# Sample value gathers behind the delta rule, norm weights spread by TensorE, later residual steps, and a pinned order of the last transposes

## The chip, the core and the metric

The kernel runs on one core of one Trainium2 chip. A core has TensorE (PE; its weight loads are shown apart as PEld), VectorE (DVE), ScalarE (ACT), GpSimd (POOL) and SyncE (SP), which work in parallel, each through its own instructions in order, and meet through semaphores. SP, ACT and POOL also issue DMA transfers. The metric is the device time of one execution in microseconds; the median of several executions is compared.

## What is computed

The reference is one step of a hybrid decoder layer for 1024 prompt tokens and for 8 sampled sequences of 4 tokens each, in float32, with a model width of 1024. Cut to what matters here:

```python
h = rmsnorm(x, norm_mix_w)
p = h @ w_in                      # q,k,v | conv input u | z | a, b | gate_A, gate_B
o_a = stick_breaking(q, k, v)     # 8 heads of 64; samples also over 256 cached positions
o_b = gated_delta(silu(conv(u)))  # 4 heads of 128, state 128x128, chunks of 64
m = sigmoid(g_a) * (o_a @ w_pa) + sigmoid(g_b) * (o_b @ w_pb)
x = x + m @ w_o
x = x + square(relu(rmsnorm(x, norm_mlp_w) @ w_up)) @ w_down
y = rmsnorm(x, norm_final_w)
```

The sampled sequences read cached keys and values through a page table (`cache_k[page_table]`, `cache_v[page_table]`): 16 pages of 128 rows, each row 512 numbers.

## The kernel before

All large products are made from three matmuls each (`dense`, L134 to L139: high part by high part, high by low, low by high), with 256 to 288 columns of tokens at a time. A planner orders the instructions: it simulates the engines, and places an instruction by its place in the program among those that it thinks ready; `tc.high_priority()` lifts a block, and `tc.issue_after(x)` puts instructions behind `x`. The order that it writes is then fixed for each engine.

The stages, in order of the program:

- **Start** (L76 to L220). Nine tiles `xn` of tokens are loaded on SP's queue, with three weight tiles `ws_u` between them and, behind the second tile, `nmb`, the mixing norm's weights broadcast to 128 partitions (L95). Five small loads go on ACT's queue, four of them into `vrow`, which TensorE transposes into `vec` (L156 to L159), from where all small weights are read. For each tile ACT squares it (L197), POOL takes the power (L199), DVE multiplies by the scale and `nmb` (L200), TensorE transposes (`xtp`, L208), and ACT and DVE split the result into `xh` and `xl`.
- **Prompt delta rule**, four heads (`gdn_head`, L386 to L571).
- **Sample delta rule** (L578 to L772). Cached keys and values are fetched by indirect gathers that POOL issues: `keys(s)` (L591) into `kg`, of which two buffers exist, followed by TensorE's transposes `dkt`; `values(s)` (L604) into `vg`, of which four exist. For sequences 0 to 3 both are called ahead of the delta rule. This stage's products of states with keys and queries, `dks` (L716 to L724), are 2 x 64 short matmuls; `dM`, `dMT` (L708 to L715) stand ahead of them. The gathered values are first read at L891.
- **Attention projections and attention** (L774 to L1144). `gate_steps` (L1032) compute the gates; the first 11 of 16 gate jobs precede the attention blocks, and the other five are cut into 20 steps and handed out as fills between attention blocks (`pipeline`, L1023). Nine residual steps (L1041) stand among the fills: each loads one tile of `x` again (`xr`), transposes it (`xrp`), and stores it transposed (`xs` to `xT_d`). The fills are listed at L1068 to L1074; a residual step follows gate steps 0, 2, 4, ..., 16.
- **Output projection, channel mixer** (L1153 to L1570).
- **Last products and final norm** (L1573 to L1636). Feature tiles of `w_down` products are added into eight tiles `ys`, in four stages of columns. For each stage the squares are summed (`sa`, and `sl` for the last feature tile), TensorE sums them over partitions (`pf`, L1618 and L1619), POOL takes the power (`fr`), and the tiles are transposed (`fin`, L1630), scaled, and stored.

Of the kernel before, what the change touches and what calls it, by code (L numbers as in the profile page):

```python
# [8 lines left out]
F32 = mybir.dt.float32  # L9
F32R = mybir.dt.float32r  # L10
I32 = mybir.dt.int32
I64 = mybir.dt.int64
AF = mybir.ActivationFunctionType
ALU = mybir.AluOpType
# [24 lines left out]
def hybrid_step(ctx, tc, x_prompt, x_sample, cache_k, cache_v, page_table, state_conv, state_ssm,  # L39
# [29 lines left out]
    def gtile(name):  # L69
        return psg.tile([P, 512], F32, tag="g", name=name)  # L70
# [7 lines left out]
    sctx = ExitStack()  # L78
    sp = pool("sp", 2, stack=sctx, side="right")
    nmb = sp.tile([P, D], F32, name="nmb", bufs=1)  # L80
    vrow = sp.tile([P, P], F32, name="vrow", bufs=1)
    nc.vector.memset(vrow, 0.0)
    nc.scalar.dma_start(vrow[8:16, :], norm_mlp_w.rearrange("o (k p) -> (o k) p", p=P))
    nc.scalar.dma_start(vrow[16:64, :], conv_w.rearrange("o j (i p) -> (o j i) p", p=P))
    nc.scalar.dma_start(vrow[64:65, :], gdn_norm_w)
    nc.scalar.dma_start(vrow[65:73, :], norm_final_w.rearrange("(k p) -> k p", p=P))
    winv = w_in[0].rearrange("(k p) n -> p k n", p=P)
    xns, w0s = [], []
    for t in range(9):
        xn = sp.tile([P, D], F32, tag="xn", name=f"xn{t}", bufs=7)  # L90
        n = P if t < 8 else NS
        SY.dma_start(xn[:n], x_prompt[0, t * P:(t + 1) * P, :] if t < 8 else x_sample.rearrange("s t d -> (s t) d"))
        xns.append(xn)
        if t == 1:
            SY.dma_start(nmb, norm_mix_w.to_broadcast([P, D]))  # L95
        if t in (1, 3, 5):
            wp = wpool if t == 1 else gw if t == 5 else sp
            st = wp.tile([P, 8, P], F32, tag="wst", name=f"ws_u0{t}", bufs=1)
            col = {1: 2048, 3: 1536, 5: 2560}[t]
            SY.dma_start(st, winv[:, :, col:col + P])  # L100
            w0s.append(st)
    ident = cst.tile([P, P], F32, name="ident")
    make_identity(nc, ident)
    ones = cst.tile([P, P], F32, name="ones")
    V.memset(ones, 1.0)
    powc = cst.tile([P, 2], F32, name="powc")
    V.memset(powc[:, 0:1], -0.5)
    V.memset(powc[:, 1:2], 0.5)

    def tr(out, in_, k=P):  # L110
        PE.transpose(out, in_, ident[:k, :k])
# [41 lines left out]
    ms_d = dr.tile([GH, 4, NC, 32, 32], F32, name="ms_d")  # L153
    tv_d = dr.tile([GH, 4, NC, 32, 32], F32, name="tv_d")

    vps = gtile("vps")  # L156
    tr(vps[:, :P], vrow)
    vec = cst.tile([P, P], F32, name="vec")
    V.tensor_copy(vec, vps[:, :P])  # L159
    mlw = vec[:, 8:16]  # L160

    def cwv(j, i):
# [29 lines left out]
    for t in range(9):  # L192
        n = P if t < 8 else NS
        c0 = t * P
        xn = xns[t]
        junk = sp.tile([P, D], F32, tag="junk", name=f"junk{t}", bufs=1)
        S_.activation(junk[:n], xn[:n], AF.Square, accum_out=sst_[:n, t:t + 1])  # L197
        V.tensor_scalar(sst_[:n, t:t + 1], sst_[:n, t:t + 1], 1.0 / D, EPS, op0=ALU.mult, op1=ALU.add)
        rpow(rstd[:n, t:t + 1], sst_[:n, t:t + 1], 0, 1)  # L199
        V.scalar_tensor_tensor(xn[:n], xn[:n], rstd[:n, t:t + 1], nmb[:n], op0=ALU.mult, op1=ALU.mult)  # L200
        cc = min(t // 2, 3)
        co = c0 - CX[cc][0]
        for hf in range(2):
            pt = (ttile, gtile)[hf](f"xtp{t}_{hf}")
            pv = pt.rearrange("p (k c) -> p k c", k=4)
            for k in range(4):
                kk = hf * 4 + k
                tr(pv[:, k, :n], xn[:n, kk * P:(kk + 1) * P], n)  # L208
            xh_ = xhc[cc][:, hf * 4:hf * 4 + 4, co:co + n]
            S_.activation(xh_, pv[:, :, :n], AF.Copy)  # L210
            V.tensor_tensor(xlc[cc][:, hf * 4:hf * 4 + 4, co:co + n], pv[:, :, :n], xh_.bitcast(F32), op=ALU.subtract)
        if t in (1, 3, 5):
            w0.append(load_w(None, f"u0{t}", gw if t == 5 else wpool, w0s[t // 2]))
    scp = sp.tile([24, 1536], F32, name="scp", bufs=1)
    nc.scalar.dma_start(scp, state_conv[0].rearrange("s j c -> (s j) c"))
    pcv = gtile("pcv")
# [387 lines left out]
    def values(s):  # L604
        vgs[s] = bk.tile([P, 2, 512], F32, tag="vg", name=f"vg{s}", bufs=4)
        for pg in range(2):
            G.indirect_dma_start(vgs[s][:, pg, :], None, cvf, bass.IndirectOffsetOnAxis(ap=idx[:, 2 * s + pg:2 * s + pg + 1], axis=0))

    for s in range(4):
        keys(s)  # L610
        values(s)
    dctx = ExitStack()
    dk = pool("dk", stack=dctx, side="right")
    blkf = blk.rearrange("p b t -> p (b t)")
# [97 lines left out]
    pmt = gtile("dmt")  # L712
    tr(pmt[:, 0:P], dM)
    dMT = dk.tile([P, P], F32, name="dMT")
    V.tensor_copy(dMT, pmt[:, 0:P])  # L715
    pks = gtile("dks")  # L716
    for i, i0 in enumerate((4, 0)):
        kz = dk.tile([P, GH, NSEQ, NS], F32, tag="big", name=f"kz{i}")
# [322 lines left out]
    def residual_step(t):  # L1041
        n = P if t < 8 else NS
        xn = ak.tile([P, D], F32, tag="xr", name=f"xr{t}", bufs=1)
        SY.dma_start(xn[:n], x_prompt[0, t * P:(t + 1) * P, :] if t < 8 else x_sample.rearrange("s t d -> (s t) d"))
        for hf in range(2):
            pv = dtile(f"xrp{t}_{hf}", True).rearrange("p (k c) -> p k c", k=4)
            xs = ak.tile([P, 4, P], F32, tag="xs", name=f"xs{t}{hf}", bufs=1)
            for k in range(4):
                kk = hf * 4 + k
                tr(pv[:, k, :n], xn[:n, kk * P:(kk + 1) * P], n)  # L1050
            S_.activation(xs[:, :, :n], pv[:, :, :n], AF.Copy)
            SY.dma_start(xT_d[hf * 4:hf * 4 + 4, :, t * P:t * P + n].rearrange("k p c -> p k c"), xs[:, :, :n])
# [16 lines left out]
    for x, (j, b) in enumerate(gjobs[11:]):  # L1069
        for c in range(len(CX)):  # L1070
            fills.append(lambda j=j, b=b, c=c: gate_step(j, b, c))
            t = 4 * x + c
            if t % 2 == 0 and t // 2 < 9:
                fills.append(lambda t=t // 2: residual_step(t))  # L1074
    pipeline(0, SPLIT, fills)
    ofb0 = zp.tile([P, 4, 256], F32, tag="zz", name="ofb0")
    SY.dma_start(ofb0, o_d[4:8, :, 0:256].rearrange("k p c -> p k c"))
# [514 lines left out]
    for c, tiles in enumerate(stages):  # L1592
        o, o2 = c * QN, c % 2 * QN
        for j in range(KT):
            cs_ = slice(j * P, (j + 1) * P)
            pt = bk2[j % 2](f"pv{c}_{j}")
            hs = hid[c // 2]
            dense(pt, [w[:, 0, cs_] for w in wd], [w[:, 1, cs_] for w in wd], [h[:, 0, o2:o2 + QN] for h in hs],
                  [h[:, 1, o2:o2 + QN] for h in hs], QN)
            yv_ = ys[j][:, o:o + QN]  # L1600
            with tc.high_priority():
                V.tensor_tensor(yv_, pt[:, :QN], yv_, op=ALU.add)
            if j == 0:
                S_.activation(sa[:, o:o + QN], yv_, AF.Square)
            else:
                sb_ = lp.tile([P, QN], F32, tag="sb", name=f"sb{c}_{j}") if j < KT - 1 else sl[:, o:o + QN]
                S_.activation(sb_, yv_, AF.Square)
                if j < KT - 1:
                    V.tensor_tensor(sa[:, o:o + QN], sa[:, o:o + QN], sb_, op=ALU.add)
            S_.activation(yv_, yv_, AF.Copy, scale=vec[:, 65 + j:66 + j])  # L1610
        with tc.high_priority():
            pf = bk2[0](f"pf{c}")
            fr = lp.tile([P, 3], F32, tag="fr", name=f"fr{c}", bufs=2)
            V.memset(fr, 1.0)
            m = len(tiles)
            for i, t in enumerate(tiles):
                n = P if t < 8 else NS
                PE.matmul(pf[:n, i:i + 1], lhsT=sa[:, t * P:t * P + n], rhs=ones[:, 0:1], start=True, stop=False)  # L1618
                PE.matmul(pf[:n, i:i + 1], lhsT=sl[:, t * P:t * P + n], rhs=ones[:, 0:1], start=False, stop=True)  # L1619
            V.tensor_scalar(fr[:, 0:2], pf[:, 0:2], 1.0 / D, EPS, op0=ALU.mult, op1=ALU.add)  # L1620
            if m == 3:
                V.tensor_scalar(fr[:NS, 2:3], pf[:NS, 2:3], 1.0 / D, EPS, op0=ALU.mult, op1=ALU.add)
            rpow(fr, fr, 0, 3)
        for i, t in enumerate(tiles):
            n = P if t < 8 else NS
            fo = lp.tile([P, D], F32, tag="fo", name=f"fo{t}")
            for hf in range(2):
                pt = (gtile, ttile)[hf](f"fin{t}_{hf}") if i < 2 else dtile(f"fin{t}_{hf}", hf == 1)
                for j in range(4):
                    tr(pt[:n, j * P:(j + 1) * P], ys[4 * hf + j][:, t * P:t * P + n])  # L1630
                if hf == 0:
                    S_.activation(fo[:n, 0:512], pt[:n], AF.Copy, scale=fr[:n, i:i + 1])
                else:
                    V.tensor_scalar(fo[:n, 512:1024], pt[:n], fr[:n, i:i + 1], None, op0=ALU.mult)
            SY.dma_start(y_prompt[0, t * P:t * P + P, :] if t < 8 else y_sample.rearrange("s t d -> (s t) d"), fo[:n])
# [27 lines left out]
```

## Time and profile before

| | us |
|---|---|
| median of three runs | 1746.8 (1742.78 to 1747.74) |
| the profiled execution | 1754.63 |
| its span, first to last instruction | 1752.9 |

The granted clock of TensorE had a mean of 0.992 over the span. A profile of one execution gives, for each engine, when each instruction ran and what released it. In its rows L-numbers are lines of the kernel; `out<-in` names tiles; `x34` is a count; `[0.61 <-issue]` is idle time ahead of an instruction and what ended it, where "issue" means that nothing which the profile shows was waited for. SPq, ACTq and POOLq are the issuing of transfers. The granted clock is the share of full speed that TensorE was allowed.

### The profile page before, as it was taken

What the parts mean: (1) busy time and instruction counts of PE and PEld (TensorE: products, weight loads), DVE (VectorE), ACT (ScalarE), POOL (GpSimd) and SP (SyncE); (2) the same over time, 40 slices, a digit from 0 to 9 for tenths busy, and PEclk for the clock granted to TensorE, in tenths of its full rate; (3) what the DMA queues carried; (4) which work ended last, traced back from release to release, by engine and by line L of the source; (5) the groups of instructions that cost most, each with busy time, mean ns of one, the idle gap of its engine ahead of it and who ended that gap; (6) DMA issues with size and microseconds to landing.
All of it is one profiled execution on the core that took longest, in us unless ns stands there. A gap on an engine that the chain in (4) does not pass through costs nothing.

```text
span 1752.9 us, 34523 instructions
## 1 busy us (share of the span) xinstructions
PE 1704.8 (97%) x13902; PEld 1645.2 (94%) x13902; DVE 1148.9 (66%) x2299; ACT 783.2 (45%) x1554; POOL 206.6 (12%) x247
## 2 busy tenths in 40 slices
PE   7999999999998999999999999999999999999998
PEld 6999999999998787887989999999999999999998
DVE  6665677868224416658857487887777678788843
ACT  5553435343323225555433355554544564444353
POOL 1110111110004125335310000000000000000000
PEclk9999999999998999999999999999999999999999
DMA  5142232234337457758223644554443666532321
GB/s 177 37 127 67 67 117 79 81 96 144 118 97 230 138 161 210 188 145 248 67 86 117 194 126 146 164 150 148 146 150 133 212 215 220 170 123 90 128 83 66
DMA packets 234219, 239.22 MB, mean 136 GB/s; under 512 B 22882, under 2 KB 192195, under 8 KB 234060
## 3 DMA queue, kind: packets, MB, share of 16 engines
q1 hardware_dynamic: 229110, 226.27, 42.4%
q0 software_dynamic: 3200, 10.52, 1.9%
q8 instruction: 109, 1.79, 0.4%
q10 hardware_dynamic: 1750, 0.23, 0.1%
q14 instruction: 50, 0.41, 0.1%
HBM read 163.21 MB, written 73.77 MB: 135 GB/s over the span
## 4 chain that ended last, share of the span: by engine, by line
PE 74%; issue 8%; DMA 6%; DVE 6%; POOL 3%; ACT 1%; SPq 1%; POOLq 0%; DVEq 0%; ACTq 0%
PE pu L139 6%; PE pu L137 6%; PE pu L138 6%; PE pw L139 4%; PE pw L138 4%; PE pw L137 4%; PE pd_g L137 2%; POOL am L938 2%; PE pd_g L139 2%; PE pd_g L138 2%; POOL s L935 1%; PE px L138 1%; PE px L137 1%; PE px L139 1%; PE pv L137 1%
## 5 line engine op out<-in xcount | busy, mean ns | idle before, releaser
L139 PE MATMUL pu<-Xh,ul 128*128 128x264 f32 x812 | 230.1, 284 | 0.0
L137 PE MATMUL pu<-Xh,uh 128*128 128x264 f32 x812 | 229.8, 283 | 0.1
L138 PE MATMUL pu<-Xl,uh 128*128 128x264 f32 x812 | 229.7, 283 | 0.0
L137 PE MATMUL pw<-hc,w 128*128 128x264 f32 x728 | 205.4, 285 | 2.4 <-ACT w L1475 2.4
L138 PE MATMUL pw<-hc,w 128*128 128x264 f32 x728 | 205.7, 286 | 0.0
L139 PE MATMUL pw<-hc,w 128*128 128x264 f32 x728 | 200.9, 285 | 1.0 <-DVE w L1476 1.0
L137 PEld LDWEIGHTS pu<-Xh,uh 128*128 128x128 f32 x812 | 153.1, 189 | 0.3 <-ACT uh L1226 0.3
L137 PE MATMUL pd_g<-xh,wh_g 128*128 128x256 f32 (+1 forms) x512 | 150.9, 295 | 1.8 <-ACT gt L1037 1.6
L138 PEld LDWEIGHTS pu<-Xl,uh 128*128 128x128 f32 x812 | 152.7, 188 | 0.0
L139 PEld LDWEIGHTS pu<-Xh,ul 128*128 128x128 f32 x812 | 152.0, 188 | 0.0
L139 PE MATMUL pd_g<-xh,wl_g 128*128 128x256 f32 (+1 forms) x512 | 149.2, 291 | 0.1
L138 PE MATMUL pd_g<-xl,wh_g 128*128 128x256 f32 (+1 forms) x512 | 148.6, 290 | 0.0
L137 PEld LDWEIGHTS pw<-hc,w 128*128 128x128 f32 x728 | 137.9, 190 | 2.6 <-ACT w L1475 2.6
L138 PEld LDWEIGHTS pw<-hc,w 128*128 128x128 f32 x728 | 137.2, 189 | 0.0
L139 PEld LDWEIGHTS pw<-hc,w 128*128 128x128 f32 x728 | 134.4, 188 | 1.4 <-DVE w L1476 1.4
L942 DVE TENSOR_TENSOR_SCAN pr<-am 128x127 f32<-128x127 f32 (+7 forms) x64 | 88.1, 1378 | 54.8 <-POOL am L938 54.8
L137 PEld LDWEIGHTS pd_g<-xh,wh_g 128*128 128x128 f32 x512 | 97.8, 191 | 7.0 <-ACT gt L1037 3.0
L139 PEld LDWEIGHTS pd_g<-xh,wl_g 128*128 128x128 f32 x512 | 97.6, 191 | 2.0 <-issue 1.9
L138 PEld LDWEIGHTS pd_g<-xl,wh_g 128*128 128x128 f32 x512 | 97.6, 191 | 0.6 <-issue 0.4
L1475 ACT ACTIVATE w<-a 128x512 fp32r<-128x512 f32 x78 | 43.5, 620 | 84.5 <-PE pw L139 74.4
L139 PE MATMUL px<-mh,wl_wo 128*128 128x264 f32 x256 | 72.2, 285 | 0.9 <-DVE wl_wo L1227 0.8
L138 PE MATMUL px<-ml,wh_wo 128*128 128x264 f32 x256 | 72.6, 285 | 0.0
(584 smaller groups left out, 5126.2 us busy)
## 6 DMA issues: line engine op xcount, KB each, us to landing
hc_d<-t SPq DMA_DIRECT2D x26, 924.0 KB
hc<-hc_d SPq DMA_DIRECT2D x87, 264.0 KB
a<-in_w_down_dram SPq DMA_DIRECT2D x48, 256.0 KB
ws_g<-in_w_in_dram SPq DMA_DIRECT2D x16, 512.0 KB
ws_wo<-in_w_o_dram SPq DMA_DIRECT2D x32, 256.0 KB
ua<-in_w_up_dram SPq DMA_DIRECT2D x16, 512.0 KB
ub<-in_w_up_dram SPq DMA_DIRECT2D x16, 512.0 KB
gA_d<-gt SPq DMA_DIRECT2D x8, 528.0 KB
```

Source lines behind the costliest of these rows:

```text
L137: PE.matmul(pt[:, :n], lhsT=wh[k], rhs=xh[k], start=(k == 0), stop=False)
L138: PE.matmul(pt[:, :n], lhsT=wh[k], rhs=xl[k], start=False, stop=False)
L139: PE.matmul(pt[:, :n], lhsT=wl[k], rhs=xh[k], start=False, stop=(k == nk - 1))
L935: G.affine_select(s[:, qsl], s[:, qsl], pattern=[[-1, P]], compare_op=ALU.is_gt, fill=0.0, base=0, channel_multiplier=1)
L938: G.tensor_scalar(am[:, :n], s[:, :n], -1.0, 1.0, op0=ALU.mult, op1=ALU.add)
L942: V.tensor_tensor_scan(pr[:, n - 1:0:-1], am_r, am_r, 1.0, op0=ALU.mult, op1=ALU.bypass)
L1475: S_.activation(tl[:, 0], src, AF.Copy)
```

## The change

Four things change.

- The broadcast load of `nmb` becomes a load of one row, `nrow`, on ACT's queue; TensorE multiplies it by a column of ones in two halves, and DVE copies these into `nmb` with priority. A first activation, `warm`, is placed at the start. For the first two tiles the multiplication by the weights is made in halves.
- The four loads into `vrow` are issued by ACT behind the Square of the second tile; `vec` is made behind the loop over tiles.
- The value gathers of sequences 0 to 3 stand behind `dMT`, and read a copy of the indices, `idxv`, which DVE makes behind it.
- Residual steps follow gate steps 3, 5, ..., 19. In the last stage the transposes of the first seven feature tiles stand ahead of the sums, and those of the eighth are issued after the last sum.

```diff
     nmb = sp.tile([P, D], F32, name="nmb", bufs=1)
+    nrow = sp.tile([1, D], F32, name="nrow", bufs=1)
+    nc.scalar.dma_start(nrow, norm_mix_w)
     vrow = sp.tile([P, P], F32, name="vrow", bufs=1)
     nc.vector.memset(vrow, 0.0)
-    nc.scalar.dma_start(vrow[8:16, :], norm_mlp_w.rearrange("o (k p) -> (o k) p", p=P))
-    nc.scalar.dma_start(vrow[16:64, :], conv_w.rearrange("o j (i p) -> (o j i) p", p=P))
-    nc.scalar.dma_start(vrow[64:65, :], gdn_norm_w)
-    nc.scalar.dma_start(vrow[65:73, :], norm_final_w.rearrange("(k p) -> k p", p=P))
...
-        if t == 1:
-            SY.dma_start(nmb, norm_mix_w.to_broadcast([P, D]))
...
+    warm = cst.tile([P, 1], F32, name="warm")
+    S_.activation(warm, ones[:, 0:1], AF.Square)
...
+    for hf in range(2):
+        pt = (dtile, gtile)[hf](f"nmb{hf}")
+        PE.matmul(pt, lhsT=ones[0:1, :], rhs=nrow[:, hf * 512:hf * 512 + 512], start=True, stop=True)
+        with tc.high_priority():
+            V.tensor_copy(nmb[:, hf * 512:hf * 512 + 512], pt)
...
-    vps = gtile("vps")
-    tr(vps[:, :P], vrow)
     vec = cst.tile([P, P], F32, name="vec")
-    V.tensor_copy(vec, vps[:, :P])
...
-        S_.activation(junk[:n], xn[:n], AF.Square, accum_out=sst_[:n, t:t + 1])
+        sq_ = S_.activation(junk[:n], xn[:n], AF.Square, accum_out=sst_[:n, t:t + 1])
+        if t == 1:
+            with tc.issue_after(sq_.ins):
+                nc.scalar.dma_start(vrow[8:16, :], norm_mlp_w.rearrange("o (k p) -> (o k) p", p=P))
+                nc.scalar.dma_start(vrow[16:64, :], conv_w.rearrange("o j (i p) -> (o j i) p", p=P))
+                nc.scalar.dma_start(vrow[64:65, :], gdn_norm_w)
+                nc.scalar.dma_start(vrow[65:73, :], norm_final_w.rearrange("(k p) -> k p", p=P))
...
-        V.scalar_tensor_tensor(xn[:n], xn[:n], rstd[:n, t:t + 1], nmb[:n], op0=ALU.mult, op1=ALU.mult)
+        for o in (0, 512) if t < 2 else (0,):
+            w = 512 if t < 2 else D
+            V.scalar_tensor_tensor(xn[:n, o:o + w], xn[:n, o:o + w], rstd[:n, t:t + 1], nmb[:n, o:o + w], op0=ALU.mult,
+                                   op1=ALU.mult)
...
+    vps = gtile("vps")
+    tr(vps[:, :P], vrow)
+    V.tensor_copy(vec, vps[:, :P])
...
-            G.indirect_dma_start(vgs[s][:, pg, :], None, cvf, bass.IndirectOffsetOnAxis(ap=idx[:, 2 * s + pg:2 * s + pg + 1], axis=0))
+            G.indirect_dma_start(vgs[s][:, pg, :], None, cvf, bass.IndirectOffsetOnAxis(ap=idxv[:, 2 * s + pg:2 * s + pg + 1], axis=0))
 
     for s in range(4):
         keys(s)
-        values(s)
+    idxv = bk.tile([P, 16], I32, name="idxv")
...
-    V.tensor_copy(dMT, pmt[:, 0:P])
+    mark = V.tensor_copy(dMT, pmt[:, 0:P])
+    with tc.issue_after(mark.ins):
+        V.tensor_scalar(idxv, idx, 0, None, op0=ALU.add)
+    for s in range(4):
+        values(s)
...
-            if t % 2 == 0 and t // 2 < 9:
-                fills.append(lambda t=t // 2: residual_step(t))
+            if t >= 3 and t % 2 and t // 2 < 10:
+                fills.append(lambda t=t // 2 - 1: residual_step(t))
...
+        m = len(tiles)
+        fins = [[(gtile, ttile)[hf](f"fin{t}_{hf}") if i < 2 else None for hf in range(2)] for i, t in enumerate(tiles)]
+
+        def fin_tr(js):
...
+        if c == 3:
+            fin_tr(range(KT - 1))
         with tc.high_priority():
             pf = bk2[0](f"pf{c}")
...
-                PE.matmul(pf[:n, i:i + 1], lhsT=sl[:, t * P:t * P + n], rhs=ones[:, 0:1], start=False, stop=True)
+                mark = PE.matmul(pf[:n, i:i + 1], lhsT=sl[:, t * P:t * P + n], rhs=ones[:, 0:1], start=False, stop=True)
...
+        if c == 3:
+            with tc.issue_after(mark.ins):
+                fin_tr([KT - 1])
+        else:
+            fin_tr(range(KT))
```

The new `fin_tr(js)` makes the transposes of the feature tiles `js` for each token tile of the stage, into PSUM tiles that are taken ahead of it for the first two token tiles.

More of the change, by code (lines that the diff above doesn't have):

```diff
@@ L1610, in hybrid_step @@
             S_.activation(yv_, yv_, AF.Copy, scale=vec[:, 65 + j:66 + j])
+        m = len(tiles)
+        fins = [[(gtile, ttile)[hf](f"fin{t}_{hf}") if i < 2 else None for hf in range(2)] for i, t in enumerate(tiles)]
+        def fin_tr(js):
+            for i, t in enumerate(tiles):
+                n = P if t < 8 else NS
+                for j in js:
+                    if fins[i][j // 4] is None:
+                        fins[i][j // 4] = dtile(f"fin{t}_{j // 4}", j >= 4)
+                    tr(fins[i][j // 4][:n, j % 4 * P:(j % 4 + 1) * P], ys[j][:, t * P:t * P + n])
+        if c == 3:
+            fin_tr(range(KT - 1))
         with tc.high_priority():
@@ L1614, in hybrid_step @@
             V.memset(fr, 1.0)
-            m = len(tiles)
             for i, t in enumerate(tiles):
@@ L1627, in hybrid_step @@
             for hf in range(2):
-                pt = (gtile, ttile)[hf](f"fin{t}_{hf}") if i < 2 else dtile(f"fin{t}_{hf}", hf == 1)
-                for j in range(4):
-                    tr(pt[:n, j * P:(j + 1) * P], ys[4 * hf + j][:, t * P:t * P + n])
+                pt = fins[i][hf]
                 if hf == 0:
```

## The prediction

> **What bounds the kernel now.** I read the page first, then the busy table over chosen stretches, TensorE's list of waits, the chain of waits at the start, and the timelines of the places that the diff touches.
>
> ```profile
> span 1752.9 us, 34523 instructions
> PE 1704.8 (97%) x13902; PEld 1645.2 (94%) x13902; DVE 1148.9 (66%) x2299; ACT 783.2 (45%) x1554; POOL 206.6 (12%) x247
> ...
> q8 instruction: 109, 1.79, 0.4%
> ```
>
> TensorE (PE) is busy 1704.8 of 1752.9 us, so only 48 us are idle. No edit here removes a matrix product; the change can win only idle time, and time in which TensorE runs at a low granted clock. Three stretches hold most of both. The columns of the next table are the stretch, its length, the busy time (and instructions) of PE, PEld, DVE, ACT and POOL, the granted clock, the DMA share and GB/s.
>
> ```profile
> 10.30:16.63 6.33, 4.19 (x18) 3.10 (x19) 5.65 (x11) 5.88 (x11) 1.53 (x3) 1.00 0.96 332
> 16.63:20.19 3.56, 3.56 (x17) 3.56 (x18) 3.56 (x7) 3.48 (x7) 0.45 (x2) 0.52 1.11 354
> 555.39:565.13 9.74, 5.43 (x66) 2.69 (x65) 0.65 (x3) 0.62 (x2) 6.36 (x7) 0.71 0.83 266
> 565.13:569.70 4.57, 4.57 (x22) 4.57 (x22) 1.31 (x2) 0.38 (x1) 0.00 (x0) 0.50 0.03 11
> 569.70:570.90 1.20, 1.20 (x11) 1.16 (x10) 0.00 (x0) 0.00 (x0) 0.00 (x0) 0.99 0.00 0
> 658.40:662.20 3.80, 0.79 (x5) 0.41 (x3) 1.17 (x3) 1.12 (x3) 1.25 (x4) 0.96 1.07 234
> 662.20:665.40 3.20, 3.14 (x12) 3.05 (x13) 0.67 (x2) 1.11 (x2) 0.00 (x0) 0.51 1.02 302
> ```
>
> Each stretch with much idle time is followed by one at about half the granted clock (0.52, 0.50, 0.51): a stall is paid for twice. The 22 gate matmuls from 565.13 took 4.57 us; the 11 after them, at 0.99, took 1.20.
>
> ```profile
> PE xtp L111 <- DVE sst__148 L198: 10.5, 2, 10.3
> PE dks L723 <- issue: 4.2, 6, 1.0
> ...
> PE xrp L111 <- DMA xr<-in_x_prompt_dram: 2.3, 1, 2.3
> PE pb L138 <- DVE obl L1122: 2.1, 2, 1.7
> ```
>
> The reader is to see that three of these waits stand exactly where the diff works: the start, the `dks` products of the sample delta rule, and the first residual step.
>
> **Part 1, the start.** The first two rows are the chain of waits (start, length, what), the others the timeline.
>
> ```profile
> 1.74 6.41 DMA nmb<-in_norm_mix_w_dram
> 8.17 7.32 DMA ws_u<-in_w_in_dram
> ...
> 5.35 0.28 ACTq L86 DMA_DIRECT2D vrow<-in_norm_final_w_dram  x1
> 5.66 1.28 ACT L197 ACT_TABLE_LOAD   x1 [5.66 <-DMA xn<-in_x_prompt_dram]
> 6.95 1.06 ACT L197 ACTIVATE junk<-xn 128x1024 f32<-128x1024 f32 x1
> 8.97 1.29 DVE L200 SCALAR_TENSOR_TENSOR xn<-xn,rstd,nmb 128x1024 f32<-128x1024 f32 x1 [0.68 <-POOL rstd L114]
> ```
>
> Two paths meet here. On SP's queue the weight load `ws_u` was issued at 8.17, just as the 512 KB broadcast `nmb` landed (1.74 + 6.41 = 8.15); it released the weight split `wh_u` at 15.5, and TensorE is dense from 16.63. On the other path ScalarE issued its fifth small load at 5.35, loaded its table from 5.66 to 6.94, and squared the first tile.
>
> Removed: 524 kB from a saturated DMA stretch, 524/0.354 = 1.5 us for everything behind it on SP's queue; from ScalarE's path the table load (1.28) and the blocked load (5.66 - 5.35 = 0.31), 1.6 us. Halving the first multiplies lets the first transposes start 0.6 us sooner (half of 1.29). So the second path gains 2.2 us and the DMA path 1.5, and the lesser counts: **-1.5 us**. Added: a 4 KB load, two products of 512 columns on an idle TensorE, two copies of 512 columns (estimate: half of the 1.29 us each) on a VectorE that does little before 8.97, and four load issues in ScalarE's stream behind the second Square. Those four cost about 1.5 us of issue and are covered by that Square (1.06) and by the wait for `ws_u`. If they block as the fifth load did here, they stand ahead of the first weight split: +2.6 us at worst. `vrow`'s transpose and copy go behind the loop; their first user, the short convolution, comes tens of us later: 0. Ends -2.2 and +2.6; the half-clock stretch (1.7 us lost of 3.56) may move or stay with either.
>
> **Part 2, the value gathers.** `dks` is made of two equal batches of 64 short matmuls. These rows are the timelines of PE, POOL and DVE, and the row of the gathered values' first use.
>
> ```profile
> 555.39 1.28 PE L723 MATMUL dks<-sst,kz 128*32 128x128 f32 x34
> 557.28 0.43 PE L723 MATMUL dks<-sst,kz 128*32 128x128 f32 x4 [0.61 <-issue]
> ...
> 572.13 1.51 PE L723 MATMUL dks<-sst,kz 128*32 128x128 f32 x46
> 543.23 2.00 POOL L607 DMA_INDIRECT vg<-in_cache_v_dram,idx  x1 [0.30 <-issue]
> ...
> 556.73 0.94 POOL L607 DMA_INDIRECT vg<-in_cache_v_dram,idx  x1 [0.30 <-issue]
> 557.69 0.60 POOL L114 TENSOR_TENSOR drk<-drk,powc 128x1 f32<-128x1 f32 x1
> 558.72 0.28 DVE L715 COPY dMT<-dmt 128x128 f32<-128x128 f32 x1
> L891 PE MATMUL dav<-vg,dw x32: 592/592/617, 618.5 to 638.2; 128*32 128x512 f32 x32
> ```
>
> The first batch ran 34 at full speed; the other 30 dripped from 557.28 to 565.13, about four at a time, with "issue" (nothing that the profile shows) before the groups, while the gathers moved. The second batch, with no DMA running, did 46 in 1.51 us, so 64 take 2.1. The first took 9.74: 7.6 us lost. Then 22 matmuls at half clock, 4.57 against 2.4: 2.2 more, 9.8 in all. I read the drip as a shortage of instructions: queue 8 moved 1.79 MB in 109 packets, 64 bytes for each of the 27,804 PE and PEld rows, so TensorE's program comes through the same DMA engines, and these were at a share of 0.83 with gathers.
>
> The edit takes eight gathers (2 MB) out of 543 to 558 and lets them wait for `idxv`, a copy of the indices made behind `dMT`. Behind the waiting gathers on POOL stand the later key gathers and two small powers; ahead go the keys of sequences 0 to 3. The power `drk` ran at 557.69 behind the last value gather and held `dMT` to 558.72; without those gathers it runs earlier, and `dMT` follows its transpose, which stands directly ahead of `dks` on TensorE. So the values issue from about 556, at 1.44 us each (ten issues, keys among them, stand between 543.23 and 557.67), until about 567; they are needed at 618.5, 50 us later: that cover is ample. But they now start **with** `dks`, and what was crowded before may be crowded behind it: 30 matmuls in 7.85 us are 0.26 each, against 0.11 for the gate products (1.20 for 11); if 5 of these 11 us go at that rate, 19 matmuls pass instead of 45, which costs 3 us. I take 9.8 - 3 = **-7 us**; ends -9.8 (stall and clock loss gone) and +3 (stall kept, later products slowed too).
>
> The Trainium skill, "Runtime: NRT & Kernel Launch", section "Instruction fetch mechanics", says that a program is streamed in 16 KiB blocks and that crossing one is mostly hidden. The block size agrees with the row (1.79 MB in 109), the hiding does not agree with my reading of the drip; by that rule this term would be 0.
>
> **Part 3, the residual steps.** The diff lists them three gate steps later.
>
> ```profile
> 650.23 0.53 SPq L1044 DMA_DIRECT2D xr<-in_x_prompt_dram  x1
> 662.26 1.94 PE L111 MATMUL xrp<-ident,xr 128*128 128x128 f32 x8 [2.35 <-DMA xr<-in_x_prompt_dram]
> ```
>
> The first load was issued at 650.23 behind the heads' loads at a DMA share above 1.0 and landed 12 us later; TensorE, in order, waited 2.35 us and then ran 3.14 us at 0.51, 1.6 lost. Gate products whose weights are already split can go first. Gain 3.9; I take **-3.5**, since the score products around it still wait a little for their own loads. All nine loads and eighteen stores move on SP's queue. At the far end the last ones (0.64 MB) come near the loads of `ofb`, whose split already held TensorE for 2.1 us (row `pb`): at 234 GB/s +2.7, the upper end.
>
> The Trainium skill's "TensorE: Matmul & The Clock Gate", section "HAM oscillation", asks for no idle gap above about 3.4 us. By that rule a gap of 2.35 would cost no clock and this term would be 2.3; the row at 0.51 disagrees, and I go by the row.
>
> **Part 4, the last feature tile.** Of its 24 closing transposes, 21 stand ahead of the sums already, and three behind.
>
> ```profile
> 1741.33 1.69 PE L111 MATMUL fin<-ident,y 128*128 128x128 f32 x14
> 1741.99 0.42 ACT L1607 ACTIVATE sl<-y 128x264 f32<-128x264 f32 x1 [1.23 <-DVE y L1602]
> 1742.99 0.96 PE L111 MATMUL fin<-ident,y 128*128 128x128 f32 x7
> 1743.79 0.28 PE L1619 MATMUL pf<-ones,sl 128*128 128x1 f32 x2
> 1744.67 0.55 PE L111 MATMUL fin<-ident,y 128*128 128x128 f32 x3
> ```
>
> That is the order which the edit pins, so it changes nothing here: **0**. At best the sums start when `sl` is ready (1742.41 instead of 1743.79, -1.4); if the pinned order delays a bank, +0.5.
>
> **Sum.** -1.5 - 7 - 3.5 + 0 = -12 us. On the profiled execution (1754.63, its span 1752.9 and 1.7 around it) that gives 1742.6. That execution is 7.8 us above the median of the runs shown, so a part of its stalls may be its own; the same 12 us off the median 1746.8 give 1734.8, and I say **1735**.
>
> **The rivals.** *A: the shortage only moves.* The values issue as `dks` starts and the next instruction blocks arrive late again; parts 1 and 3 alone remain: 1746.8 - 5 = 1741.8. For it: key gathers, gate stores and weight loads still move then. Against: 2 MB fewer are queued when `dks` begins. The Trainium skill's rule on instruction fetch ("Runtime: NRT & Kernel Launch") ends in the same place.
>
> *B: the change does not do what it says.* The four small loads block ScalarE ahead of the weight split (+2.6) and the gathers give nothing, so that the residual steps alone win: 1746.8 + 2.6 - 3.5 = 1745.9. For it: the fifth small load waited 2.6 us here. Against: by then the earlier ones have landed.
>
> *C: slower.* POOL's order puts the eight waiting values ahead of the keys of sequences 2 and 3. These then start at 567 instead of right behind `drk` (558.3), and TensorE, in order, stands before their transposes: 8.7 us of wait and 3.4 us at half clock, with parts 1 and 3: 1746.8 + 8.7 + 1.7 - 5 = 1752.2. With part 1 at its upper end instead it is 1756.3, and I put C at 1753. It decides as soon as value gathers precede a key gather whose transposes were placed early. Against it: the keys stand first in the program.
>
> **How the numbers follow.** Forecast 0.48 (1730 to 1739), A 0.30 (1739 to 1745), B 0.14 (1743 to 1749), C 0.08 (above 1749). 0.3% of 1746.8 is 5.2 us, about what a measurement of this kernel can tell from no change. Faster than 1741.6: the forecast and 0.4 of A, 0.60. Slower than 1752.0: most of C and a little of B, 0.07. The rest, 0.33, is within. The range runs from 1730 (all three parts near their best ends) to 1746 (B's middle); it leaves out half of B, C and a little below.
>
> **What would show it.** Right: no "issue" before `dks` and about 2 us for each batch; a granted clock of 1.0 from 559 to 570; value gathers of POOL behind the copy of `dMT`; TensorE dense before 15.5 us; no wait of `xrp` for `xr`. Wrong: the same four-at-a-time drip at `dks` or just behind it; ScalarE idle before the first weight split; waits of `dkt` for key gathers; a longer wait of `pb` for `obl`.

## The result, and the profile after

| | us (median) | runs |
|---|---|---|
| before | 1747.27 | 1740.68 to 1749.88, 6 runs |
| after | 1755.79 | 1752.9 to 1757.45, 6 runs |
| ratio after / before | 1.0055 | 95% interval 1.0035 to 1.0076 |
| profiled execution of after | 1754.95 | span 1753.2 |

The changed kernel is slower by 0.55%, about 9 us; 1735 had been predicted. The profiled execution of before (1754.63) stood 7.4 us above the median of its kernel, that of after (1754.95) stands 0.8 below its own. The two profiles can therefore not be subtracted from each other, although their spans are nearly the same.

The page of after, its span and busy times:

```profile
span 1753.2 us, 34533 instructions
PE 1705.3 (97%) x13906; PEld 1644.4 (94%) x13906; DVE 1153.4 (66%) x2304; ACT 784.7 (45%) x1557; POOL 206.0 (12%) x247
```

TensorE has four products more (the two halves of `nmb`) and is idle as long as before, 48 us. But the waits are others. TensorE's list of waits in after; the columns are who waits for what, us in all, times, the longest:

```profile
PE sc L949 <- ACT s L951: 3.8, 1, 3.8
PE nmb L110 <- DMA nrow<-in_norm_mix_w_dram: 3.4, 1, 3.4
PE pd_g L141 <- ACT xs L1068: 3.4, 2, 1.8
PE dkt L115 <- DMA kg<-in_cache_k_dram,idx: 2.6, 2, 1.3
...
PE pb L142 <- DVE obl L1139: 2.4, 1, 2.4
...
PE xtp L115 <- DVE xn L209: 1.7, 2, 1.3
```

The waits at which the change aims are gone or smaller: that of `dks`, that of `xrp` for `xr`, and that of `xtp` for the first tile, of whose 10.5 us 1.7 are left, with 3.4 us of the new products `nmb` for their load ahead of it. In their place stand waits for ScalarE in the attention stage: scores (`sc`) wait for the copy `s` of an earlier score, gate products (`pd_g`) for the copy `xs` of a residual tile. Neither was in the list of before with more than 0.2 us.

And the stall at `dks` is indeed gone. This is the view of the tile `dks` in after (kinds of idle time would stand under the line on the engine; there is none):

```profile
L740 PE MATMUL dks<-sst,kz x128: 272/273/298, 548.6 to 559.3; 128*32 128x128 f32 x128
its engine sat idle before it (us, times) until:
who waited for it (us, times):
```

The 128 products took 10.7 us with other work between them, in place of some 20 before (555.4 to 575.6). So two named stalls left the trace and the third shrank, and the kernel got slower: the question of the experiments.

### The profile page after: what moved, and what is told of

Same layout as the page of the kernel before. It is cut to its first block, busy times and chain, and to the rows that moved or that the text cites. A ratio compares the mean times of both kernels' runs of the same rounds, so it can differ in the third digit from the quotient of the medians.

```text
span 1753.2 us, 34533 instructions
## 1 busy us (share of the span) xinstructions
PE 1705.3 (97%) x13906; PEld 1644.4 (94%) x13906; DVE 1153.4 (66%) x2304; ACT 784.7 (45%) x1557; POOL 206.0 (12%) x247
## 4 chain that ended last, share of the span: by engine, by line
PE 80%; DMA 9%; DVE 5%; ACT 3%; issue 1%; SPq 1%; POOL 0%; DVEq 0%; POOLq 0%; ACTq 0%
PE pu L143 6%; PE pu L142 6%; PE pu L141 6%; PE pw L141 5%; PE pw L142 5%; PE pw L143 5%; PE pd_g L141 3%; PE pd_g L142 3%; PE pd_g L143 3%; PE wt L115 2%; DMA xT_d<-xs 2%; PE po L997 2%; PE px L142 1%; PE px L141 1%; PE px L143 1%
```

## The experiments

Eighteen runs were made, each beside the kernel before. The kernel before took 1754 us in the comparisons of s1 to s8 and 1746 us in the later ones, so ratios are set beside each other mainly within one comparison (s1 to s4, s5 to s8, s9 to s12, s13 to s16, s17 and s18).

### The parts alone

s1 is the kernel before, unaltered. s2, s3 and s4 each have one part of the change's diff: the start (all of its hunks up to `scp`), the value gathers (`idxv` and its copy), the residual steps. For s3 and s4 these are the lines:

```diff
 s3
+    mark = V.tensor_copy(dMT, pmt[:, 0:P])
+    with tc.issue_after(mark.ins):
+        V.tensor_scalar(idxv, idx, 0, None, op0=ALU.add)
 s4
-            if t % 2 == 0 and t // 2 < 9:
-                fills.append(lambda t=t // 2: residual_step(t))
+            if t >= 3 and t % 2 and t // 2 < 10:
+                fills.append(lambda t=t // 2 - 1: residual_step(t))
```

> The kernel before, unchanged, for a second profiled execution and for the scatter of the comparison. The profiled execution of before (1754.6 us) was some 7 us above the median of its other runs (1747.3). Theory R (the residual steps cost the time): the stall at the products of states with keys is of every execution, so this profile shows it again: several rows of dks with 'issue' ahead of them, the first batch near 9.7 us long. Rival V (the stall was that execution's own): a batch of about 2.1 us, no 'issue' row, and a span near 1745; then the value gathers had little to win in most executions. The ratio is 1.000 within 0.002 by either.

> The kernel before with the start of the change alone. Both traces are level again by 60 us, so theory R expects 0 (within 2 us). Rival O (the planner's new order for the whole program, and no part by itself, makes the difference): a few us in either direction, found in places far behind the start.

> The kernel before with only the value gathers of sequences 0 to 3 moved behind dMT. Theory R: faster by 5 to 9 us, with no 'issue' before dks. Rival V (the stall was not usual): within 2 us. A third, W (the waiting gathers delay the heads' loads of keys and queries, and the score products wait): slower by 2 to 5 us, with a wait of sc of more than 2 us near 650.

> The kernel before with only the residual steps behind gate steps 3, 5, ..., 19. Theory R (ScalarE copies a residual tile out of PSUM in its order and waits there for the store of the one before; the gate products behind it wait for the bank, and the last steps stand beside the loads of ofb and the split of obl): slower by 6 to 10 us, lost between 680 and 910, with waits of pd_g for xs and a last xs behind 795. Rival V: 0 to 3 us faster, since the first xr is no longer waited for (2.35 us in the profile of before).

| | ratio | 95% interval |
|---|---|---|
| s1 before | 0.9991 | 0.9977 to 1.0005 |
| s2 start | 1.0028 | 1.0013 to 1.0043 |
| s3 value gathers | 1.0037 | 1.0022 to 1.0053 |
| s4 residual steps | 0.9982 | 0.9967 to 0.9997 |

The first theory, that the residual steps cost the time, fell at once: they are the part that wins, 0.18%, some 3 us. The start and the gathers lose, and the three sum to 0.47%, near the change's 0.55%.

The profile of s1 has 0.6 us of "issue" at `dks`, where before had 4.2, and 3.7 us of it at the gate products `pd_g`. So the size and the place of that stall differ between executions of one program.

### Inside the start, and the gathers further back

s5 adds one line to the kernel before, s6 has only the late `vec` of the change's start, s7 only the `nmb` made by TensorE. s8 is s3 with the copy of the indices one step further back.

```diff
 s5
+    warm = cst.tile([P, 1], F32, name="warm")
+    S_.activation(warm, ones[:, 0:1], AF.Square)
 s8, against s3
-    mark = V.tensor_copy(dMT, pmt[:, 0:P])
+    V.tensor_copy(dMT, pmt[:, 0:P])
...
-    V.tensor_scalar(dqs, pks[:, P:2 * P], decg, None, op0=ALU.mult)
+    mark = V.tensor_scalar(dqs, pks[:, P:2 * P], decg, None, op0=ALU.mult)
```

> The kernel before with one addition: the first activation warm at the start (it loads ScalarE's table early). Nothing else differs, yet the order that the planner writes for TensorE differs: from the 42nd product on, some 2000 of the 13046 products stand in another order. Theory O (the start alone was slower since the planner wrote another order behind it, which leaves TensorE idle and at half clock in other places): level or ahead by up to 1.5 us at 60 us, and then a shift of the whole time of some us of either sign (beyond 0.1%), from places far behind the start. Rival S (the start's own work costs the 5 us): within 1 us of before, since one activation costs nothing.

> The kernel before with only the four loads of vrow behind the second Square and vec behind the loop. Theory O: a shift of some us of either sign, from places behind 60 us. Rival S: +2 to +5 us, visible as idle time of TensorE in the first 60 us or at the first user of vec.

> The kernel before with only nmb spread by TensorE instead of the broadcast load (no halves, no warm, the small loads as before). Theory O: TensorE dense some 1.5 us earlier at the start, level by 60 us, then a shift of some us of either sign. Rival S: +3 to +5 us, present at 60 us already.

> As the run with the value gathers alone, but the copy of the indices waits for the reading of the second dks batch, so that no value gather is in flight beside dks. Theory F (while gathers are in flight TensorE's instructions arrive late, and short products suffer most): no drip in dks, its 128 products in about 5 us in place of 13 to 20, a smaller drip in the gate products behind it, and 4 to 9 us faster than the run with the values alone, 0 to 3 faster than before. Rival N (the drip has nothing to do with the gathers): dks takes as long as in the run with the values alone, and the time is within 2 us of it.

| | ratio | 95% interval |
|---|---|---|
| s5 warm | 1.0001 | 0.9988 to 1.0014 |
| s6 late vec | 1.0037 | 1.0019 to 1.0056 |
| s7 nmb by TensorE | 1.0008 | 0.9995 to 1.0021 |
| s8 gathers behind dks | 0.9961 | 0.9943 to 0.9979 |

Theory F held in its direction: with no value gather beside `dks` the kernel is 0.39% faster than before. In s8 the value gathers are issued from 571.59 on, and `dks` lies from 555.5 to 566.1 with 0.3 us of "issue", against 556.3 to 576.6 with 6.3 us of it in s3. But the gain is larger than F had said: 0.76% or 13 us against s3 (4 to 9 expected), and some 7 us against before (0 to 3 expected). All waits of "issue" in TensorE's lists come to 8.6 us in s3 and 2.4 in s8, so they explain about half of the 13 us, set across two comparisons; the rest is open. Theory O did not show itself in s5: a new order, and no change of time. The late `vec` looked like the culprit. In the whole change it was not, as the next comparisons show.

### The whole change, taken apart

s9 is the changed kernel, s10 the same without the start, s11 the changed kernel with the gathers where s8 has them, s12 is s10 with the gathers there.

> The changed kernel, unaltered, beside the kernel before on one chip and beside the next three runs. All theories: about +0.55% of before (1.0035 to 1.0076 before). The profile is for stage-by-stage comparison with the next runs.

> The change without its first part (value gathers, residual steps and last tile only). If the parts add, as measured alone: values +0.37%, residual -0.18%, last tile 0: +0.2% of before, 0.3% faster than the whole change. If the start's cost was only chance of the planner's order in that kernel: as slow as the whole change, +0.55%.

> The whole change, with the copy of the indices placed behind the reading of the second dks batch instead of behind dMT. Theory F (gathers in flight starve TensorE of instructions; alone the later place was worth 0.76%): 0.5% to 0.8% faster than the whole change, so -0.2% to +0.05% of before. Rival P (in the whole change dks already runs without a row of 'issue', so the place of the gathers costs nothing there, and the loss lies in the start and in the order behind): within 0.2% of the whole change.

> A candidate for the best version: the kernel before with the residual steps of the change, the gathers behind dks and the pinned last tile, without the start. If the parts add: -0.18% and -0.39%, so -0.5% to -0.6% of before, some 10 us. If both win the same idle time near 650 (the first residual tile is late there in the run with the gathers behind dks: xrp waited 2.9 us): -0.4%.

| | median, us | ratio | 95% interval |
|---|---|---|---|
| s9 whole change | 1753.68 | 1.0041 | 1.0024 to 1.0057 |
| s10 without the start | 1742.69 | 0.9982 | 0.9968 to 0.9996 |
| s11 gathers further back | 1749.72 | 1.0023 | 1.0011 to 1.0035 |
| s12 without start, gathers further back | 1741.17 | 0.9976 | 0.9961 to 0.9991 |

All the loss hangs on the start: with it the change loses 0.41%, without it the same three other parts win 0.18%. The start, predicted at -1.5 us, makes a difference of 11.0 us (1753.68 - 1742.69). That is more than twice what the start alone cost in s2 (0.28%, 4.9 us), so its own work is unlikely to be all of it. s11 stays within 0.2% of s9, as rival P had it, and not F; their intervals overlap. s12 is faster than the kernel before and the changed kernel, but by 0.24%, less than either expectation, and its interval overlaps that of s10.

Where the 11 us lie is read from the busy table over chosen stretches; its columns are the stretch, its length, the busy time (and instructions) of PE, PEld, DVE, ACT and POOL, the granted clock, the DMA share and GB/s. First s10:

```profile
0.00:60.00 60.00, 46.78 (x358) 44.64 (x359) 39.20 (x73) 30.74 (x56) 10.10 (x22) 1.00 0.48 147
60.00:540.00 480.00, 473.68 (x3958) 468.51 (x3959) 297.23 (x753) 189.76 (x431) 55.49 (x50) 1.00 0.33 100
540.00:640.00 100.00, 97.65 (x863) 82.46 (x862) 33.24 (x76) 33.10 (x65) 33.67 (x33) 0.98 0.59 177
640.00:700.00 60.00, 57.71 (x459) 52.77 (x458) 33.82 (x33) 30.45 (x65) 19.71 (x32) 1.00 0.81 210
700.00:780.00 80.00, 80.00 (x672) 71.46 (x673) 47.82 (x46) 43.52 (x97) 31.26 (x43) 1.00 0.62 165
```

Then s9, the whole change:

```profile
0.00:60.00 60.00, 50.91 (x362) 46.23 (x363) 41.35 (x78) 31.02 (x57) 10.13 (x22) 1.00 0.45 138
60.00:540.00 480.00, 471.18 (x3928) 465.15 (x3928) 302.46 (x754) 193.38 (x434) 54.97 (x53) 1.00 0.33 102
540.00:640.00 100.00, 96.36 (x846) 79.77 (x845) 29.77 (x73) 30.92 (x61) 31.65 (x30) 1.00 0.56 167
640.00:700.00 60.00, 55.66 (x448) 51.49 (x447) 31.71 (x31) 25.60 (x58) 22.98 (x30) 1.00 0.67 173
700.00:780.00 80.00, 78.80 (x646) 68.92 (x646) 47.98 (x46) 44.77 (x99) 31.32 (x43) 1.00 0.69 183
```

Idle is length less busy. In the first 60 us s9 is idle 4.1 us less, but the products of `nmb` fill nearly all of that. From 60 to 780 us s9 is idle 8.8 + 3.6 + 4.3 + 1.2 = 17.9 us, s10 6.3 + 2.4 + 2.3 + 0 = 11.0: seven of the eleven microseconds, in small pieces, **all of them behind the stretch that the start's edits touch**. Most of the rest is longer busy time: up to 840 us in s9 and 830 us in s10 TensorE ran nearly the same number of products (6626 and 6631) and was busy 807.6 and 800.8 us, of which the products of `nmb` are 3.75. Behind that the two take 910.3 and 909.9 us. Why the busy time is some 3 us longer is not shown.

What these pieces are is seen in ScalarE's timeline around 650 us (start, length, what, idle time ahead of it and what ended it). s9:

```profile
657.03 1.06 ACT L131 ACTIVATE wh_g<-ws_g 128x1024 fp32r<-128x1024 f32 x1 [5.51 <-DMA ws_g<-in_w_in_dram]
657.99 0.93 ACT L951 ACTIVATE s<-sc,sbb 128x256 f32<-128x256 f32 x2
...
688.39 0.60 ACT L1068 ACTIVATE xs<-xrp 128x512 f32<-128x512 f32 x1 [3.66 <-DMA xT_d<-xs]
```

and TensorE's there:

```profile
658.50 0.50 PE L949 MATMUL sc<-kh,qs 128*128 128x512 f32 x1 [3.05 <-ACT s L951]
...
689.04 0.39 PE L141 MATMUL pd_g<-xh,wh_g 128*128 128x256 f32 x1 [1.29 <-ACT xs L1068]
```

ScalarE, in order, stood 5.51 us before a weight split whose load had not landed; the copy `s`, which would free a bank for the next score, was queued behind it, and TensorE stood 3.05 us. At 688.39 the same: `xs` has one buffer, its copy waits until the tile before is stored, and the gate product waits for the bank. In s10 the load of that split, the 13th of the gate weights, was issued at 634.99 instead of 645.84, and the split waits for TensorE instead, which does not hold TensorE up:

```profile
645.07 1.06 ACT L127 ACTIVATE wh_g<-ws_g 128x1024 fp32r<-128x1024 f32 x1 [2.68 <-PE pd_g L138]
```

The long wait of this split alone is not the loss. In s5 it waits 6.68 us for its load, yet TensorE's list of waits has none for `s`, and the kernel loses nothing: there the copy behind the split is one of a gate product. It costs where TensorE needs the copy that is queued behind it.

### The same order without the start's edits

The orders of TensorE's products can be compared by their rows in the traces, in order of time and with line and buffer numbers left out; there are 13902 (13906 with `nmb`). The expectations count the products of the program instead, 13046.

| one kernel | the other | first row that differs | rows found in the same order |
|---|---|---|---|
| before | s5 (one activation) | the 41st | 11589 |
| before | s10 | the 4436th | 12819 |
| before | the change | the 1st | 10954 |
| the change | s13, s14 | within the first 9 | 13803, 13788; all differences among the first 356 |

So one activation at the start is enough to re-order much of what follows: the last row that differs between before and s5 runs at about 757 us. s13, which is s10 with that activation, has the changed kernel's order behind the first 356 rows (about 57 us) without any of its work at the start. s14 is the whole change with `vec` made early. s15 and s16 are the two halves of s6 on the kernel before: the loads late, and the transpose late. In s15 the transpose stands ahead of the loads, so `vec` holds zeros there and the small weights are left out of the computation.

> The change without its start, with the first activation warm alone added. Behind the first 500 products TensorE's order is the same as in the whole change. Theory O2 (the order costs): as slow as the whole change, +0.4% of before within 0.1. Rival D (the start's own edits cost, above all the late vec): as fast as the change without the start, -0.2% within 0.1. Half of each would lie at +0.1%.

> The whole change, but the four loads of vrow and the making of vec where the kernel before has them. Same order of TensorE behind the first 500 products as the whole change. Rival D: 0.3% to 0.6% faster than the whole change, so -0.2% to +0.1% of before, and the wait of pd_uv for upv near 58 us is back at 1.1 us (2.0 in the whole change). Theory O2: within 0.15% of the whole change.

> The kernel before with only the four loads of vrow issued behind the second Square; vec is made at its old place in the program. If the late loads are what makes the late vec slow (ScalarE's stream ahead of the weight splits): +0.3% to +0.4%, and at most +0.1% in the next run. Theory O2 and a cost of the transpose: within 0.1% of before.

> The kernel before with the loads of vrow as they were and only the transpose and copy into vec placed behind the loop over tiles. If the late transpose (and the evictions that are queued behind it) is what costs: +0.3% to +0.4%, with a wait of pd_uv for upv of 2.0 us; otherwise within 0.1%.

| | ratio | 95% interval |
|---|---|---|
| s13 other three parts, and warm | 1.0039 | 1.0024 to 1.0055 |
| s14 change, vec early | 1.0040 | 1.0025 to 1.0056 |
| s15 loads late | 1.0015 | 1.0002 to 1.0028 |
| s16 transpose late | 0.9987 | 0.9976 to 0.9998 |

s13 has nothing of the start but the activation `warm` and loses as much as the whole change; s14 has all of it but the late `vec`, and loses the same. **Within the whole change the rest of the start's edits cost nothing that can be measured; the order that the planner writes once anything at the start differs costs 0.6%** (0.39% against -0.18%, in two comparisons). TensorE's list of waits in s13:

```profile
...
PE pd_g L139 <- ACT xs L1057: 3.3, 2, 1.7
PE pb L140 <- DVE obl L1128: 3.0, 2, 2.4
PE sc L938 <- ACT s L940: 3.0, 2, 2.2
PE dkt L113 <- DMA kg<-in_cache_k_dram,idx: 2.5, 2, 1.3
```

These are the waits of the changed kernel. The same view of s10:

```profile
...
PE sc L936 <- DMA kh<-kh_d: 3.2, 2, 2.0
PE pb L138 <- DVE obl L1126: 2.4, 1, 2.4
...
PE dkt L111 <- DMA kg<-in_cache_k_dram,idx: 1.1, 1, 1.1
...
PE sc L936 <- ACT s L938: 0.5, 1, 0.5
```

No wait of `pd_g` for `xs`, 0.5 us of `sc` for `s`. Both directions of s15 and s16 speak against the late `vec` as a cost of its own: one half lost 0.15%, the other won 0.13%, where together they had lost 0.37% in s6. Why s6 lost that is not settled.

Nor is the order alone the cause of every difference here. In the traces s2, s5, s6, s7, s15 and s16 have one and the same order behind the first 356 rows, the one that s5 brings, and yet they lie from 0.9987 to 1.0037; s5 and s6 differ by 0.36% within one comparison. Without the other parts that order costs nothing in s5.

### With which part the order costs, and the gathers again

s17 is s4 with the activation `warm`; s18 is s3 once more.

> The kernel before with the residual steps of the change and the activation warm, which brings the other order of TensorE. If that order costs through the residual steps (pd_g waits for xs, as in the whole change): +0.2% to +0.4% of before, with waits of pd_g for xs of some 3 us. If it costs through the value gathers: -0.2% to 0.

> The run with the value gathers alone once more, on another occasion. Firm: +0.2% to +0.5%, with the drip in dks and a wait of xrp near 680. If the earlier result belonged to its occasion (the kernel before took 1754 us there, and 1746 on two later ones): within 0.15% of before.

| | ratio | 95% interval |
|---|---|---|
| s17 residual steps, and warm | 1.0013 | 1.0001 to 1.0025 |
| s18 value gathers | 0.9975 | 0.9961 to 0.9989 |

s17 fell between the two expectations: the order costs something with the residual steps alone (`pd_g` waits 2.3 us for `xs` there), and more with the gathers too. The lists of waits point the same way: the wait of `pd_g` for `xs` is there with the residual steps alone, while those of `sc` for `s` (0.8 us in s17, 3.0 in s13) and of `dkt` for `kg` (none in s17, 2.5 in s13) grow or appear when the gathers are moved too. How the time divides is open.

s18 is the surprise: the program of s3, which had lost 0.37%, wins 0.25%. The timelines of TensorE show why. s3:

```profile
556.34 0.62 PE L727 MATMUL dks<-sst,kz 128*32 128x128 f32 x10
...
562.00 0.43 PE L727 MATMUL dks<-sst,kz 128*32 128x128 f32 x4 [0.99 <-issue]
563.44 0.43 PE L727 MATMUL dks<-sst,kz 128*32 128x128 f32 x4 [1.00 <-issue]
564.86 0.43 PE L727 MATMUL dks<-sst,kz 128*32 128x128 f32 x4 [0.99 <-issue]
566.99 0.59 PE L727 MATMUL dks<-sst,kz 128*32 128x128 f32 x3 [1.70 <-issue]
```

s18, the same instructions in the same order, with the value gathers issued beside them as well (the first at 559.75):

```profile
558.66 0.62 PE L727 MATMUL dks<-sst,kz 128*32 128x128 f32 x10
...
559.47 0.42 PE L727 MATMUL dks<-sst,kz 128*32 128x128 f32 x6
...
560.08 0.84 PE L727 MATMUL dks<-sst,kz 128*32 128x128 f32 x18
...
561.66 1.07 PE L727 MATMUL dks<-sst,kz 128*32 128x128 f32 x30
...
566.49 1.96 PE L727 MATMUL dks<-sst,kz 128*32 128x128 f32 x64
```

No drip, that is, no groups of about four products with "issue" between them. Waits of "issue" of 0.3 to 6.3 us at `dks`, `pd_g` or `dkt` in the sample stage stand in the profiles of s1 to s8, where the kernel before took 1754 us, and in that of before, which took 1754.63. The profiles of after, s9 to s14 and s18 have none, those of s15 to s17 only 0.5 to 1.0 us ahead of scores. s1 to s4 and s13 to s16 are on record with the same chip number, 9, so if the number means the same chip, the chip is not what differs.

## Why the prediction was wrong

**The step that failed** is the one behind the sum: every term was read from the order of the trace of before, as if what stood behind an edit would stay where it was. The kernel's order is written by a planner from simulated times, and an edit at the start gives another one from there to about 757 us, in the attention stage. The prediction named no such rival. By s9 and s10, parts 2 to 4 together won 3.0 us instead of 10.5, and the start, put at -1.5, made the kernel 11.0 us slower, through the order. The measured 1755.8 lies close to the prediction's slower case C (1753), but by another mechanism, so that is chance. Term by term:

- **Part 1 (-1.5, ends -2.2 and +2.6).** At the start it is about as predicted: in after TensorE's first feature product starts at 14.88, and they are dense from 15.60, where 15.5 was named and before has 16.63. The half-clock stretch is not gone: the feature products from 15.98 to 18.33 start 0.21 us apart, like the 22 in 4.57 us at 0.50, though the busy table gives a granted clock of 1.00 for them. So the stretch most likely only lies earlier: that of before ran from 16.63 to 20.19. But nothing of the gain is left at 60 us. The first row is of before, from TensorE's timeline:

```profile
59.86 0.39 PE L137 MATMUL pd_uv<-xh,wh_u 128*128 128x256 f32 x1 [1.12 <-ACT upv L346]
```

 and this of after:

```profile
59.86 0.39 PE L141 MATMUL pd_uv<-xh,wh_u 128*128 128x256 f32 x1 [1.96 <-ACT upv L359]
```

 Both restart at 59.86: ScalarE's copy `upv`, queued behind the convolution's activation, sets that moment, and a faster start only waits longer for it. The term was 0 instead of -1.5. What the start then brought with the other parts in place, +0.6%, is no end of its range at all, since the range held only the start's own costs.

- **Part 2 (-7 of a stall of 9.8).** The mechanism was there in part: in s3 the drip stands beside the value gathers, and in s8, with them moved off, it is gone; s18 has the gathers and no drip. So the stall most likely belonged to the kind of execution that had been profiled, and the times to be predicted were of the other kind; no profile of before from that other kind was taken. The prediction had the hint in its hand ("7.8 us above the median of the runs shown, so a part of its stalls may be its own") and used it only for the offset; the stall of 9.8 us and the surplus of 7.8 may well be the same thing. Where the drip exists, the move behind `dMT` shifted it and lost 0.37% (s3): rival A, and worse. Where it doesn't, the gathers won 0.25% (s18); from where is not settled. In the whole change a place further back gave another 0.18% (s11 against s9), which is not clear of noise.

 The Trainium skill, "Runtime: NRT & Kernel Launch", section "Instruction fetch mechanics", says that crossing a block of instructions is mostly hidden. s18, without such waits, agrees with it; s3, with the same program, would not if its drip is a shortage of instructions, and that is not shown.

- **Part 3 (-3.5).** Right in sign and size: s4 is at -0.18%, 3 us, and `xrp` no longer waits for `xr`. The feared end, a longer wait of `pb` for `obl`, came to 4.0 us in s4 and 2.4 in after, against 2.1 before. What the step missed is the single buffer of `xs`: in the other order `pd_g` waits for it (3.4 us in after, 3.3 in s13, 2.3 in s17), in s10's it does not.

- **Part 4 (0).** Right: in after 15 transposes, the first sums, 6 transposes, the last sums and 3 transposes follow one another, nearly the order of before. It ran only together with other parts.

- **Rival C** did occur in small: POOL issued the values (549.27 to 558.52) ahead of the later keys (from 559.77) in after, and TensorE waited at the transposes of keys, but 2.6 us and not 8.7.

## What to carry to other kernels

Where a planner writes the order, first make an edit that does nothing at the same place, and time that: here one activation took the change without its start from 0.18% faster to 0.39% slower, more than any part was meant to win. An edit is better judged against kernels of the same order, though even those lay 0.36% apart here (s5 and s6). Before a stall is priced, ask whether the execution that was profiled is like those that were timed; a profile that stands above its kernel's median by about the size of the stall is a warning. And weight splits and the copies that free PSUM share ScalarE's order here, so a split planned ahead of its load's landing can stop TensorE (3.05 us in s9), however little ScalarE is busy (45%).

## What the runs showed of the hardware

The same program met the same gathers and ran at very different speed. The busy table of s3 and of s18 over the stretch of `dks` and the gathers; s3:

```profile
556.00:570.00 14.00, 7.57 (x80) 4.58 (x79) 0.67 (x3) 2.16 (x4) 9.18 (x10) 0.83 0.70 203
```

s18:

```profile
558.00:570.00 12.00, 12.00 (x187) 10.30 (x186) 3.45 (x6) 3.84 (x7) 9.26 (x10) 1.00 0.72 212
```

DMA share and rate were alike (0.70 and 0.72, 203 and 212 GB/s), yet 80 products passed in 14 us in the one and 187 in 12 us in the other. A busy DMA is thus not enough for the drip; what makes the two kinds of execution differ is open, and the prediction's reading of it as a shortage of instructions is still only argued.

The granted clock did not follow the length of a gap. In s9:

```profile
655.45:658.50 3.05, 0.00 (x0) 0.00 (x1) 0.38 (x1) 1.47 (x3) 0.00 (x0) 1.00 0.86 332
658.50:662.00 3.50, 3.50 (x25) 3.33 (x26) 3.01 (x5) 1.98 (x5) 3.22 (x6) 1.00 0.46 125
801.90:804.32 2.42, 0.00 (x2) 0.00 (x1) 2.36 (x2) 0.41 (x1) 2.42 (x2) 0.88 1.04 210
804.32:807.10 2.78, 2.78 (x13) 2.56 (x15) 2.65 (x3) 0.00 (x0) 2.69 (x5) 0.50 1.07 276
807.10:810.50 3.40, 3.40 (x24) 3.07 (x25) 3.40 (x7) 0.68 (x2) 1.81 (x2) 0.50 1.09 241
```

A gap of 3.05 us cost no clock, one of 2.42 us was followed by half the clock for the next 6 us. Where a gap lies seems to matter. The half-clock stretches of s9 ahead of the end, 59.63 to 63.05 and 803.74 to 810.56, lie on a grid of 3.41 us. In the cell ahead of the first, 56.22 to 59.63, TensorE was busy 1.47 us. The longer gap is split between two cells, 653.55 to 656.96 and 656.97 to 660.38, in which TensorE was busy 1.90 and 1.88 us; the shorter one lies mostly in one, 800.33 to 803.74, in which it was busy 1.57 us, and half the clock began at the end of that cell. Three cases of one trace don't make a rule. The prediction's rule that each long stall is paid for twice holds often, not always. The Trainium skill's "TensorE: Matmul & The Clock Gate", section "HAM oscillation", puts the limit at idle gaps above about 3.4 us: the first gap agrees with it, the second does not.
